# Late modulation tiles moved to the input projection's end, a rotation one product later, and the first up-weight casts ahead of the last squares

## The chip, the cores and the metric

The kernel runs on one core of one Trainium2 chip. The metric is device time in microseconds (us), the median of several executions; lower is better. Engines go by the names of the profile: PE (TensorE, matrix products and transposes), DVE (VectorE), ACT (ScalarE), POOL (GpSimd), SP (SyncE, which here only starts transfers). Each engine takes its instructions strictly in the order in which they were written into its queue, and an instruction that waits for another engine or for a transfer holds up everything behind it on its own engine.

## The reference

One block of a hybrid network on 512 latent tokens of width 2048 and 256 context tokens, everything in f32. Cut to what this change touches:

```
mod = silu(c) @ w_ada + b_ada                 # 6 vectors of 2048: the modulation
h   = rms_norm(x) * (1 + sc_a) + sh_a
p   = h @ w_in                                # input projection: q_a, kv_a, k_rope, conv columns
q   = rms_norm(q_a) @ w_q_b                   # 8 heads: 128 plain + 64 rotated columns
k,v = rms_norm(kv_a) @ w_kv_b                 # and the same for the context tokens
att = softmax(q k^T * scale) v                # 768 keys: 512 latent, 256 context
mix = group rms_norm(concat(att, gated conv))
x   = x + gt_a * (mix @ w_out)                # output projection, residual
hf  = rms_norm(x) * (1 + sc_f) + sh_f
u   = dwconv3(hf @ w_up);  x = x + gt_f * ((a * silu(g)) @ w_down)
```

The modulation's later vectors (`gt_a`, `sh_f`, `sc_f`, `gt_f`) are not needed before the output projection's residual.

## The kernel before, in words

Activations lie transposed, 128 features on the partitions and tokens along the free axis. PE multiplies a reduced-precision f32 kind, so each operand is split into a high and a low part and each product is three matmuls (`mm3`, lines 189, 190 and 191: high times high, high times low, low times high). A weight block is therefore loaded by SP into a raw tile, its high part is made by a cast on ACT (line 168) and its low part by a subtraction on DVE (line 169). The line 191 matmul is the one that needs the low part.

**The stages**, in the time of the profiled execution: the input projection runs to about 390 us (weights `rw`, split into `w_0`, `w_4`, `w_8`; products `pp`); the queries of head pair 0 and the context tiles follow (raw weights `rq`, split parts `wq00`, `wq02`, `wq01`; raw `rc`, split parts `wc..`); attention runs from about 433 to 627 us; the output projection to about 810; then `up` begins with a part called `uf` (raw weights `ufr`, split parts `ufw0`, `ufw1`, ... and, for rows 3 to 5, `ufw_0`/`ufw_512`).

**Late modulation tiles.** `w_ada` comes in tiles of 128 x 2048, one for each 128 outputs. Tiles 32 to 87 of it are done late: a tile is loaded by `late_load`, and DVE multiplies it with `silu(c)` and sums, either as two halves (line 266, two instructions; a tile in the raw buffers `ra`) or at once (line 270; a tile in the buffers `ada`). `late_both` does the dot of the tile loaded last and loads the next. Before the change they are spread over the attention (one tile a step, tiles `ra`) and the output projection (tiles `ada`).

**Attention.** `steps` are the 32 pairs of a head and a group of 128 queries. Step n makes the scores of step n+2 (PE, `s`, lines 741 to 745), the row maximum of step n+2's scores (DVE `mn`, line 756), the exponentials of step n+1 (ACT `p`, line 759), the transposes of step n's exponentials (PE `t`, line 772; their high part by ACT into `pth`, line 775, their low part by DVE into `ptl`, line 776), and every second step the product with the values (PE `po`, lines 189 to 191), whose result ACT copies out (`o`, line 788). Sums, scalings and their broadcasts (PE `gb`, line 309; DVE `o`, line 814, and `acc`, line 384) are put between. In the last steps the first weights of the output projection (`ofr`, two loads at steps 29 and 30) are fetched and split (`ofw_0`, `ofw_4`, `ofw_8`), and tiles of x (`x`, line 820) are loaded.

**Rotation.** `q_nope(0, i)` makes one of pair 0's three query products; the third (i = 2, `pq` from `wq02`) is copied out by ACT as `xq` (line 663), then rotated: one PE product with a permutation matrix (`qr`, line 389) and DVE work. The order of the calls is i = 0, 2, 1.

**From the output projection to up.** The last two rows of the output are done in two halves of the tokens (`ol`, weights `o14..`, `o15..`). After each half `residual` adds the result to x (DVE, line 1004) and squares it (ACT `fq`, line 364; DVE `fq0t`, line 365). `rms_steps` turns the squares into the norm: matmuls `rs` over the squares (line 326), a root on ACT and a reciprocal on DVE (`rr`, lines 299 and 301), and a broadcast by transposes on PE (`rs`, line 309). `hf_tile` then makes up's operands `hf` (ACT lines 983, 986 and 965; DVE lines 982, 987 and 966).

**What sets the order.** The program is written as Python loops; a scheduler with a simulated timeline then decides the order on each engine. `keep` pins an instruction to its place in the program, and `tc.issue_after` adds a dependency that holds an instruction back until another one. Buffers come from pools with a fixed number of places, so a load also waits until the last readers of its place are done. Small generators (`bg`, `pump`) let background work be issued between products.

## Time and profile before

| | us |
|---|---|
| median of 3 runs | 2130.95 (2128.15 to 2133.67) |
| profiled execution, time | 2127.2 |
| profiled execution, span | 2125.4 |
| PE busy in the span | 2080.8 (98%) |
| DVE busy in the span | 1823.5 (86%) |
| ACT busy in the span | 1049.7 (49%) |

The span goes from the first to the last instruction, and 1.8 us of the execution's time lie around it. Sums below are made against the profiled execution; the median lies 3.75 us above it. PE is idle for 2125.4 - 2080.8 = 44.6 us in the whole span. A time in a row of the timeline is an instruction's start, the number behind it its duration, and a bracket names how long the engine had been idle before it and what ended that. Durations of matmuls overlap: the distance of two starts tells what one costs.

### The profile page before, as it was taken

The numbers are of one execution on the slowest core, as the hardware profiler recorded it, in microseconds if no ns is written. First come the engines' busy times: TensorE is split into PE (matmuls) and PEld (weight loads), VectorE is DVE, ScalarE is ACT, GpSimd is POOL, SyncE is SP. The second block draws the span as 40 slices with busy tenths as digits, with TensorE's granted clock in tenths as the row PEclk, the third lists the DMA queues.
The fourth block names the chain that finished last, engine by engine and source line by source line (L and its number), as shares of the span: only waits on it lengthen the run. The fifth ranks groups of instructions, "written<-read, shape, count | busy, mean of one in ns | idle before, by whom it ended". The sixth has DMA issues, their size and how long they took to land.

```text
span 2125.4 us, 35175 instructions
## 1 busy us (share of the span) xinstructions
PE 2080.8 (98%) x13268; PEld 1873.8 (88%) x13268; DVE 1823.5 (86%) x2952; ACT 1049.7 (49%) x1715; POOL 116.7 (5%) x144
## 2 busy tenths in 40 slices
PE   7999999999989999999999999999999999999997
PEld 4788788889978889999999999999999889999997
DVE  7998987778897878898999999999999759888887
ACT  5533333555552337565555555555555433333445
POOL 0000000000000000011000000000000000000000
PEclk9999999999999999999999999999999999999999
DMA  9979885345558966587788788788788989877684
GB/s 329 349 275 325 277 273 192 127 143 194 207 219 318 351 254 183 143 218 205 230 240 235 225 238 237 228 236 240 225 232 246 336 309 308 261 233 235 207 248 139
DMA packets 165135, 513.74 MB, mean 242 GB/s; under 512 B 18402, under 2 KB 22754, under 8 KB 154850
## 3 DMA queue, kind: packets, MB, share of 16 engines
q1 hardware_dynamic: 128324, 418.14, 57.8%
q0 software_dynamic: 17408, 59.25, 14.2%
q10 hardware_dynamic: 19232, 34.09, 4.2%
q8 instruction: 104, 1.70, 0.3%
q14 instruction: 67, 0.55, 0.1%
HBM read 464.22 MB, written 46.14 MB: 240 GB/s over the span
## 4 chain that ended last, share of the span: by engine, by line
PE 94%; DVE 2%; ACT 2%; DMA 2%; issue 0%; SPq 0%; DVEq 0%; ACTq 0%
PE pp L189 4%; PE pp L191 4%; PE pp L190 4%; PE o L190 1%; PE o L189 1%; PE o L191 1%; PE d L189 1%; PE d L190 1%; PE d L191 1%; PE uf L189 1%; PE uf L191 1%; PE uf L190 1%; PE of L189 1%; PE of L190 1%; PE of L191 1%; PE pf L190 1%
## 5 line engine op out<-in xcount | busy, mean ns | idle before, releaser
L1167 POOL DMA_DIRECT2D u_s<-in_w_up x80 | 68.6, 857 | 682.2 <-DMA u_s<-in_w_up 312.2
L168 ACT CAST w_0h<-rw 128x512 fp32r<-128x512 f32 (+1 forms) x63 | 38.5, 618 | 108.4 <-PE pp L190 64.6
L270 DVE SCALAR_TENSOR_TENSOR ada<-ada,sv 128x2048 f32<-128x2048 f32 x32 | 73.3, 2289 | 19.7 <-DMA ada<-in_w_ada 19.7
L243 DVE SCALAR_TENSOR_TENSOR ada<-ada,sv 128x1024 f32<-128x1024 f32 x64 | 77.6, 1220 | 3.5 <-DMA ada<-in_w_ada 3.5
L540 DVE SCALAR_TENSOR_TENSOR ada<-ada,svc 128x1024 f32<-128x1024 f32 x64 | 76.0, 1221 | 2.8 <-DMA ada<-in_w_ada 2.7
L169 DVE TENSOR_TENSOR w_0l<-rw,w_0h 128x512 fp32r<-128x512 f32 (+1 forms) x63 | 42.7, 684 | 20.6 <-ACT w_0h L168 20.5
L266 DVE SCALAR_TENSOR_TENSOR ra<-ra,sv 128x1024 f32<-128x1024 f32 x48 | 57.0, 1218 | 0.1
L1281 DVE TENSOR_TENSOR u<-u,u_s 128x1024 f32<-128x1024 f32 x40 | 48.8, 1219 | 1.4 <-DMA u_s<-in_w_up 1.3
L1282 DVE TENSOR_TENSOR u<-u,u 128x1024 f32<-128x1024 f32 x40 | 48.7, 1217 | 0.0
L804 POOL TENSOR_TENSOR gr<-gr,half 128x8 f32<-128x8 f32 x4 | 9.6, 2390 | 631.0 <-DVE gr L803 631.0
L1091 DVE TENSOR_TENSOR tp<-a,tp 128x256 fp32r<-128x256 f32 x90 | 37.7, 419 | 3.0 <-ACT tp L1090 3.0
L775 ACT CAST pth<-t 128x384 fp32r<-128x384 f32 x64 | 28.9, 485 | 20.7 <-PE t L772 20.7
L1090 ACT CAST tp<-a 128x256 fp32r<-128x256 f32 x90 | 35.7, 404 | 5.2 <-DMA yl6h<-y_d 3.9
L1054 ACT ACTIVATE g<-g 128x512 f32<-128x512 f32 x43 | 27.3, 634 | 18.2 <-DVE g L1048 17.9
L551 DVE TENSOR_TENSOR acc<-acc,pp 128x512 f32<-128x512 f32 x50 | 34.2, 684 | 2.1 <-PE pp L191 2.1
L776 DVE TENSOR_TENSOR ptl<-t,pth 128x384 fp32r<-128x384 f32 x64 | 33.2, 550 | 2.3 <-ACT pth L775 2.2
L756 DVE TENSOR_REDUCE mn<-s 128x1 f32<-128x768 f32 x32 | 30.4, 952 | 4.4 <-PE s L745 4.4
L1046 ACT ACTIVATE g<-cg,sm 128x512 f32<-128x512 f32 x40 | 32.6, 816 | 0.0
L1046 ACT ACTIVATE a<-ca,sm 128x512 f32<-128x512 f32 x40 | 32.1, 802 | 0.0
L759 ACT ACTIVATE p<-s,mn 128x768 f32<-128x768 f32 x32 | 29.3, 914 | 3.3 <-DVE mn L756 2.9
L1047 DVE SCALAR_TENSOR_TENSOR g<-cg,sm,g 128x511 f32<-128x511 f32 x40 | 29.8, 745 | 0.0
L1048 DVE SCALAR_TENSOR_TENSOR g<-cg,sm,g 128x511 f32<-128x511 f32 x40 | 29.8, 745 | 0.0
(10238 smaller groups left out, 8906.4 us busy)
## 6 DMA issues: line engine op xcount, KB each, us to landing
ada<-in_w_ada SPq DMA_DIRECT2D x128, 512.0 KB, 5.7
u<-in_w_up SPq DMA_DIRECT2D x120, 512.0 KB, 8.9
w<-t_d SPq DMA_DIRECT2D x161, 256.0 KB, 5.3
u_s<-in_w_up SPq DMA_DIRECT2D x80, 512.0 KB, 3.9
u_s<-in_w_up POOLq DMA_DIRECT2D x80, 512.0 KB, 9.6
ada<-in_w_ada SPq DMA_DIRECT2D x32, 1024.0 KB, 7.0
t_d<-tp ACTq DMA_DIRECT2D x126, 256.0 KB, 5.9
v<-in_w_dnw SPq DMA_DIRECT2D x72, 384.0 KB, 5.3
```

The source lines that it names most:

```text
L169: V.tensor_tensor(out=lo[:, :n], in0=raw[:, a:a + n], in1=hi[:, :n].bitcast(F32), op=ALU.subtract)
L189: PE.matmul(ps, w[0], x[0], start=first, stop=False, skip_group_check=on_top)
L190: PE.matmul(ps, w[0], x[1], start=False, stop=False, skip_group_check=on_top)
L191: PE.matmul(ps, w[1], x[0], start=False, stop=last, skip_group_check=on_top)
L243: V.scalar_tensor_tensor(out=r, in0=r, scalar=1.0, in1=vec[:, i * 1024:(i + 1) * 1024], op0=ALU.mult, op1=ALU.mult, accum_out=col[:, i:i + 1])
L266: keep(V.scalar_tensor_tensor(out=halves[i], in0=halves[i], scalar=1.0, in1=svs[i], op0=ALU.mult, op1=ALU.mult, accum_out=lc[:, t % 4:t % ...
L270: keep(V.scalar_tensor_tensor(out=r, in0=r, scalar=1.0, in1=sv, op0=ALU.mult, op1=ALU.mult, accum_out=mod[:, t:t + 1]))
L540: keep(V.scalar_tensor_tensor(out=raw[q], in0=raw[q], scalar=1.0, in1=svc[:, q * 1024:(q + 1) * 1024], op0=ALU.mult, op1=ALU.mult, accum_o ...
L1046: A.activation(u, src, AF.Identity, bias=s("fb", m), scale=s("fw", 86 + m))
L1167: G_.dma_start(r[-1], src[more], accum_op=ALU.add)
L1281: V.tensor_tensor(out=a11, in0=a11, in1=s1, op=ALU.add)
L1282: V.tensor_tensor(out=a12, in0=a12, in1=a11, op=ALU.add)
```

## The change

Five edits:

- Two late tiles are loaded and done in the last part of the input projection (steps i = 20, 21, 22 of its third pass), as halves in buffers of their own (`ae`).
- In attention, late tiles are loaded up to step 24 only (before: up to step 27), so three tiles fewer are done there. Two are the ones above; one more falls to the output projection, whose late work is held back until the last `ptl` subtraction.
- The rotation of pair 0 is called after all three query products (i = 0, 2, 1), not inside the second.
- `residual` of the last half row is held behind the first casts of up's weights and behind an earlier `hf` tile; the norm's last squares and root are written after the first two rows of up's weights, and the `rs` matmuls are pinned in their place.
- The split parts of up's first three rows get their places before the loads are written (`pair4`).

```diff
@@ rms_steps
-    def rms_steps(sqs, n, a, width, dst, wait=0, one=False, hold=False):
+    def rms_steps(sqs, n, a, width, dst, wait=None, one=False, hold=False, pin=False):
...
+                if pin:
+                    keep(ins)
@@ input projection, third pass
+                    if 20 <= i <= 22:
+                        late_both((lambda t: ada_tiles(p_sb, 4, w_ada[t], f"ae{t}")) if i < 22 else None)
@@ q_nope
             A.copy(out=xq, in_=ps)
+            if pr:
+                q_rope(pr, xq)
+            else:
+                q_rope_0.append(xq)
+
+        q_rope_0 = []
+
+        def q_rope(pr, xq):
             rope(xq, sml(f"qr{pr}"), f"qr{pr}")
...
         for i in (0, 2, 1):
             q_nope(0, i)
+        q_rope(0, q_rope_0[0])
@@ attention steps
-            elif (at >= 2 or n >= 24) and n < 28:
+            elif (at >= 2 or n == 24) and n <= 24:
                 late_load(ada_raw)
@@ output projection, rows from OUT_EARLY on
-        late_both(ada_spare)
+        with tc.issue_after(ptl_last[0]) if k == OUT_EARLY else ExitStack():
+            late_both(ada_spare)
@@ last half rows
-            residual(NK - 2 + i, whole(raws[i], mix, f"o{NK - 2 + i}{h}", pso[i], HS[h], ld=ada_spare), HS[h])
+            ps = whole(raws[i], mix, f"o{NK - 2 + i}{h}", pso[i], HS[h], ld=ada_spare)
+            if (h, i) != (1, 1):
+                residual(NK - 2 + i, ps, HS[h])
+        if h == 1:
+            break
...
@@ up's first rows
+    pair_of = {}
+    for k in range(3):
+        pair_of[k] = pair4(f"ufw{k}")
...
-    held = [first_weights(k, k > 2) for k in range(EARLY)]
-    for k in range(3, EARLY):
-        hf_tile(k, H0)
+    held = [first_weights(k) for k in range(2)]
+    first_two = last_hi[0], last_lo[0]
+    with tc.issue_after(last_hi[0]), tc.issue_after(hf_last[0]):
+        residual(NK - 1, ps, HS[1])
+    one_bank[0] = in_turn([6])
+    bg.append(rms_steps(fsq, D, T // 2, T // 2, rl, wait=(1, 1), one=True, pin=True))
+    held += [first_weights(k, k > 2) for k in range(2, EARLY)]
+    with tc.issue_after(first_two[0]), tc.issue_after(first_two[1]):
+        for k in range(3, EARLY):
+            hf_tile(k, H0)
```

From line 300 on, line numbers in the rows of the changed kernel are larger by 4 to 27 than those of the same code before. In the rows below a name with a number behind an underscore is one buffer; `x3` at a row's end stands for three alike in a row.

**Input projection's end, DVE.** Before, from the first split of the last weight tile (`w_30`) to the low part of the first query weight (`wq00l`):

```order
L169 TENSOR_TENSOR w_30_0l<-rw_30_3298,w_30_0h 128x512
L348 TENSOR_TENSOR qa2l<-acc_574,qa2h 128x512
L551 TENSOR_TENSOR acc_686<-acc_686,pp_28_3203 128x512
L348 TENSOR_TENSOR qa3l<-acc_583,qa3h 128x512
L169 TENSOR_TENSOR w_30_4l<-rw_30_3298,w_30_4h 128x512
L354 TENSOR_TENSOR hc_3294<-cr_3291,hc_3294 128x256
L525 TENSOR_TENSOR cr_3361<-cg_3355,rc 128x256
L525 TENSOR_TENSOR cr_3367<-cg_3355,rc 128x256
L169 TENSOR_TENSOR w_30_8l<-rw_30_3298,w_30_8h 128x256
L354 TENSOR_TENSOR hc_3364<-cr_3361,hc_3364 128x256
L169 TENSOR_TENSOR wq00l<-rq_3413,wq00h 128x512
```

And the same place now, from the first low part of the normed `q_a` (`qa0l`):

```order
L352 TENSOR_TENSOR qa0l<-acc_529,qa0h 128x512
L266 SCALAR_TENSOR_TENSOR ae_3185,mod<-ae_3185,sv 128x1024
L266 SCALAR_TENSOR_TENSOR ae_3187,lc<-ae_3187,sv 128x1024
L169 TENSOR_TENSOR w_30_4l<-rw_30_3310,w_30_4h 128x512
L352 TENSOR_TENSOR qa1l<-acc_537,qa1h 128x512
L352 TENSOR_TENSOR qa2l<-acc_574,qa2h 128x512
L352 TENSOR_TENSOR qa3l<-acc_583,qa3h 128x512
L169 TENSOR_TENSOR w_30_8l<-rw_30_3310,w_30_8h 128x256
L358 TENSOR_TENSOR hc_3306<-cr_3303,hc_3306 128x256
L529 TENSOR_TENSOR cr_3373<-cg_3367,rc 128x256
L529 TENSOR_TENSOR cr_3379<-cg_3367,rc 128x256
L169 TENSOR_TENSOR wq00l<-rq_3425,wq00h 128x512
```

One pair of dots stands here, the other pair stands earlier, right behind the addition of `pp_27`; both are ahead of `wq00l`, and one `hc` moved behind it.

**The same place, ACT.** Before, around the copy of the product to be rotated (`xq`) and the casts of context weights (`wc_0h`):

```order
L347 CAST q00h<-pq_3423 128x512
L168 CAST wc_0h<-rc_3530 128x512 x3
L663 COPY xq_3457<-pq_3444 128x512
L347 CAST qro0h<-xq_3457 128x512
L168 CAST wc_0h<-rc_3530 128x512
L347 CAST q01h<-pq_3477 128x512
```

Now:

```order
L168 CAST wc_0h<-rc_3542 128x512
L530 ACTIVATE cr_3415<-cr_3415,modc,scc_3407 128x256
L357 CAST hc_3412<-cr_3409 128x256
L357 CAST hc_3418<-cr_3415 128x256
L351 CAST q00h<-pq_3435 128x512
L168 CAST wc_0h<-rc_3542 128x512
L669 COPY xq_3469<-pq_3456 128x512
L351 CAST q01h<-pq_3475 128x512
```

Before, three of the four casts from one context tile stand ahead of `xq`; now all four do.

**Attention's end, ACT.** Before, from the output copy (`o`) that the profile shows at about 600 us:

```order
L788 COPY o_5715<-po_5716 128x256
L775 CAST pth_5689<-t_5757 128x3x128
L775 CAST pth_5689<-t_5763 128x3x128
L759 ACTIVATE p_5794,den_5520<-s_5770,mn_5792 128x768
L775 CAST pth_5796<-t_5798 128x3x128
L775 CAST pth_5796<-t_5804 128x3x128
L759 ACTIVATE p_5847,den_5520<-s_5811,mn_5845 128x768
```

Now, from the same copy:

```order
L804 COPY o_5724<-po_5725 128x256
L168 CAST ofw_0h<-ofr_5876 128x512
L168 CAST ofw_4h<-ofr_5876 128x512
L168 CAST ofw_8h<-ofr_5876 128x512
L168 CAST ofw_0h<-ofr_5917 128x512
L791 CAST pth_5699<-t_5763 128x3x128
L791 CAST pth_5699<-t_5769 128x3x128
L773 ACTIVATE p_5796,den_5534<-s_5775,mn_5794 128x768
```

Four casts of output weights, which before stood behind the last `p` and two more `pth`, are now ahead of the casts and the exponentials of three steps. On DVE `ofw_0l` and `ofw_4l` stand likewise ahead of the row maximum of the step before the last, and `ofw_8l` and the next `ofw_0l` ahead of the `ptl` behind it.

**Up's start, ACT.** Before, from the cast of the third operand:

```order
L986 CAST hf2h<-x_4957 128x256
L983 ACTIVATE x_5008<-x_5008,mod,fs_7562 128x256
L364 ACTIVATE fq_7494<-x_5790 128x256
L983 ACTIVATE x_5104<-x_5104,mod,fs_7571 128x256
L1039 CAST ufw0h<-ufr_7514 128x768
L299 ACTIVATE rr<-rs,eps 128x2
L1039 CAST ufw1h<-ufr_7520 128x768
```

Now:

```order
L1003 CAST hf2h<-x_4969 128x256
L1062 CAST ufw0h<-ufr_7519 128x768
L1062 CAST ufw1h<-ufr_7523 128x768
L368 ACTIVATE fq_7528<-x_5792 128x256
L1062 CAST ufw2h<-ufr_7532 128x768
L1000 ACTIVATE x_5020<-x_5020,mod,fs_7566 128x256
L351 CAST ufw_0h<-ufr_7536 128x512
L1000 ACTIVATE x_5118<-x_5118,mod,fs_7575 128x256
L351 CAST ufw_512h<-ufr_7536 128x256
L351 CAST ufw_0h<-ufr_7546 128x512
L351 CAST ufw_512h<-ufr_7546 128x256
L351 CAST ufw_0h<-ufr_7556 128x512
```

The casts `ufw0h` and `ufw1h` come right behind `hf2h`, and the root `rr` now stands one row behind this, past the casts of rows 3 to 5. On PE the four `rs` matmuls over the squares, which stood ahead of the first `uf` product, now stand inside the third row of them, and both broadcasts behind that row.

More of the change, by code (lines that the diff above doesn't have):

```diff
@@ L310, in spread @@
         return ins.ins
-    def rms_steps(sqs, n, a, width, dst, wait=0, one=False, hold=False):
+    def rms_steps(sqs, n, a, width, dst, wait=None, one=False, hold=False, pin=False):
+        wait = wait or (0, 0)
         ng = width // P
@@ L320, in rms_steps @@
             pb = ps[:, 256:]
-        for _ in range(wait):
+        for _ in range(wait[0]):
             yield
@@ L330, in rms_steps @@
         rsqrt(r, ps[:, :ng], n)
-        for _ in range(wait):
+        for _ in range(wait[1]):
             yield
@@ L760, in softmax @@
             return pt
+        ptl_last = []
         def transposes(st, pt):
@@ L775, in transposes @@
                 A.copy(out=hi, in_=trv)
-                V.tensor_tensor(out=ptl[:, 3 * u:3 * u + 3, bs], in0=trv, in1=hi.bitcast(F32), op=ALU.subtract)
+                ptl_last[:] = [V.tensor_tensor(out=ptl[:, 3 * u:3 * u + 3, bs], in0=trv, in1=hi.bitcast(F32), op=ALU.subtract).ins]
         def attend(hd, half):
@@ L1019, in block_kernel @@
         for i in range(2):
-            residual(NK - 2 + i, whole(raws[i], mix, f"o{NK - 2 + i}{h}", pso[i], HS[h], ld=ada_spare), HS[h])
+            ps = whole(raws[i], mix, f"o{NK - 2 + i}{h}", pso[i], HS[h], ld=ada_spare)
[3 more added lines that the diff above has]
+            break
         one_bank[0] = in_turn([6 * h])
-        bg.append(rms_steps(fsq, D, h * T // 2, T // 2, rl, wait=2, one=True))
-        if h == 0:
-            bg.append(hf_early())
+        bg.append(rms_steps(fsq, D, h * T // 2, T // 2, rl, wait=(2, 2), one=True))
+        bg.append(hf_early())
     assert late["t"] == late["end"] and late["raw"] is None
@@ L1034, in block_kernel, with pair4, split4 @@
     last_hi, last_lo = [], []
-    def split4(src, n, nm):
-        hi = rw.tile([P, 1024], F32R, tag="wh", bufs=3, name=nm + "h")
-        lo = rw.tile([P, 1024], F32R, tag="wl", bufs=3, name=nm + "l")
+    def pair4(nm):
+        return [rw.tile([P, 1024], F32R, tag="w" + z, bufs=3, name=nm + z) for z in "hl"]
+    def split4(src, n, nm, pair=None):
+        hi, lo = pair or pair4(nm)
         last_hi[:] = [A.copy(out=hi[:, :n], in_=src).ins]
@@ L1155, in first_weights @@
             return [part(w[g // 4], g % 4) for g in range(G)]
-        w = split4(raw[:, :G * P], G * P, f"ufw{k}")
+        w = split4(raw[:, :G * P], G * P, f"ufw{k}", pair_of.pop(k, None))
         return [part(w, g) for g in range(G)]
@@ L1552, in block_kernel @@
     sqs.append(add_squares(None, acc2[zb.m + 1][:, H0], T // 2, "eqb", a=0))
-    bg.append(rms_steps(sqs, D, 0, T // 2, rl, wait=1, one=True, hold=True))
+    bg.append(rms_steps(sqs, D, 0, T // 2, rl, wait=(1, 1), one=True, hold=True))
     outs = final(0, rl[:, HS[0]])
```

## The prediction

> **What bounds the kernel now.** I read the page's engine line first, then PE's waits, then windows and timelines around the places that the change touches.
>
> ```profile
> PE 2080.8 (98%) x13268; PEld 1873.8 (88%) x13268; DVE 1823.5 (86%) x2952; ACT 1049.7 (49%) x1715; POOL 116.7 (5%) x144
> ...
> PE po L189 <- DVE ptl L776: 5.3, 2, 3.1
> ...
> 610.00:620.00 10.00, 6.92 (x41) 6.11 (x41) 9.26 (x20) 5.96 (x13) 0.00 (x0) 0.83 0.60 195
> 620.00:630.00 10.00, 6.88 (x38) 6.39 (x37) 8.93 (x16) 8.01 (x17) 0.00 (x0) 0.83 0.38 134
> ```
>
> PE bounds the kernel: it is idle for 44.6 us of 2125.4. No edit takes a product away, so only these idle times and slow clock can change. Behind the span, PE, weight loads, DVE and ACT busy, the window rows give the granted clock: in the 20 us around attention's end PE is busy for 6.9 of 10, its clock is 0.83, and DVE is busy for 9 of 10. PE's largest wait, on `ptl`, lies there. That is the place with most to win; waits on `xq` and on the last squares, quoted below, are the other two targets.
>
> **Attention's end.** The next rows are from the timelines of PE, ACT and DVE, from the chain of waits, and from the view of the tile `ofr`.
>
> ```profile
> 601.33 1.04 PE L309 MATMUL gb<-io,gr 128*128 128x128 f32 x8
> ...
> 603.20 0.65 PE L309 MATMUL gb<-io,gn 128*128 128x128 f32 x4 [0.18 <-DVE o L814]
> 604.54 0.50 PE L741 MATMUL s<-kl31h,q31h 128*128 128x512 f32 x1 [0.69 <-ACT p L759]
> ...
> 609.32 1.17 PE L772 MATMUL t<-io,p 128*128 128x128 f32 x6
> 611.36 0.65 PE L309 MATMUL gb<-io,gn 128*128 128x128 f32 x4 [0.88 <-DVE ptl L776]
> ...
> 615.05 0.39 PE L189 MATMUL po<-pth,v30h 128*128 128x256 f32 x1 [2.21 <-DVE ptl L776]
> ...
> 616.87 0.41 PE L189 MATMUL po<-pth,v32h 128*128 128x256 f32 x1
> 617.09 0.41 PE L190 MATMUL po<-ptl,v32h 128*128 128x256 f32 x1
> ...
> 623.24 0.55 PE L189 MATMUL po<-pth,v30h 128*128 128x256 f32 x1 [3.12 <-DVE ptl L776]
> ```
>
> ```profile
> 599.79 0.37 ACT L788 COPY o<-po 128x256 f32<-128x256 f32 x1 [2.35 <-PE po L191]
> 602.73 0.86 ACT L775 CAST pth<-t 128x384 fp32r<-128x384 f32 x2 [2.57 <-PE t L772]
> ```
>
> ```profile
> 593.66 1.22 DVE L266 SCALAR_TENSOR_TENSOR ra<-ra,sv 128x1024 f32<-128x1024 f32 x1
> ...
> 602.41 0.74 DVE L814 SCALAR_TENSOR_TENSOR o<-o,sm,gb 128x512 f32<-128x512 f32 x1
> ...
> 613.30 1.22 DVE L266 SCALAR_TENSOR_TENSOR ra<-ra,sv 128x1024 f32<-128x1024 f32 x1
> 614.44 0.55 DVE L776 TENSOR_TENSOR ptl<-t,pth 128x384 fp32r<-128x384 f32 x1
> ```
>
> ```profile
> 614.55 4.20 DMA ofr<-in_w_out_first
> ...
> 619.39 0.27 ACT o L788
> ...
> 621.37 0.60 DVE mx1l L348
> ...
> 622.63 0.48 DVE ptl L776
> ```
>
> ```profile
> DMA to landing us min/median/max: 4.3/5.5/8.0
> ```
>
> What goes: the idle of five waits, 0.18 + 0.69 + 0.88 + 2.21 + 3.12 = 7.1 us. With it goes the slow clock: from 616.2 to 620.1 and from 623.2 to 626.4, about 7.0 us of busy PE, a product of 256 columns starts 0.22 us after the one before (616.87, 617.09), against the 0.12 of the rows at 809 below. At 0.12 to 0.22 these 7.0 us hold 3.9 us of work, so 3.1 are lost. Together 10.2 us.
>
> What frees them: three tiles' dots, six instructions at 1.14 us (613.30 to 614.44) or 6.9 us of DVE, all ahead of the `ptl` that PE waits for.
>
> What comes instead: the `ofr` loads now wait for dots that end earlier, and their casts stand ahead of attention's own work on ACT and DVE. I lay this on the times of before. Both dots of the last tile now stand where one stood (593.66), so everything behind 594.80 starts 1.14 later, and the first `ofr` is issued at 596.0; at 4.25 us (the 4.20 row, the 4.3 of the tile view) it has landed at 600.3. Its three casts (0.52 each, by the ACT rows of the rotation below) end by 601.9, ahead of the `pth` casts of 602.73. The second `ofr` waits for the next dot, to about 598.7; it lands at 603.0 and its cast holds ACT to 603.6, so the two `pth` and the `p` behind it come 0.9 us late. On DVE two low parts (0.60 each, as `mx1l`) begin when the first cast is through (600.9) and end at 602.1; the row maximum and the third low part bring it to 603.6, where `o` begins, 1.2 us later than 602.41. So `gb` waits 0.18 + 1.2 = 1.4, and `s`, with `p` 0.9 late, 0.5 behind it.
>
> Then the tail. At 611.36 and 615.05 the dots were the last to come (613.30 and 614.44 are the end of that chain); without them I leave 0.6 of 3.1. The last wait's chain goes from the output copy at 619.39 to the end of `ptl` at 623.11, 3.7 us, and only `mx1l` leaves it: 3.1, under which PE has ten transposes and broadcasts, 1.2 us at a product's 0.12: 1.9 remain. New idle: 1.4 + 0.5 + 0.6 + 1.9 = 4.4; each of the four waits adds some 0.15 for the signal between engines (`hf2h` to `ufw0h` to `uf` below: 811.24 + 0.81 = 812.05 and 812.11 is the least of it), so I take 5.0. **Gain 10.2 - 5.0 = 5.2 us.** The bounds: without the new waits at the two early places it is 7.1; with a landing of 8.0 in place of 4.25 it is 5.2 - 3.75 = 1.5.
>
> The third tile goes to the output projection, one dot among DVE work that its consumers need 2 us or more later: 0. If that cover were gone it would cost its 2.3 us.
>
> **Input projection's end.**
>
> ```profile
> 379.50 0.43 DVE L169 TENSOR_TENSOR w_8l<-rw,w_8h 128x256 fp32r<-128x256 f32 x1 [0.58 <-PE pp L191]
> ...
> 388.91 0.43 DVE L354 TENSOR_TENSOR hc<-cr,hc 128x256 fp32r<-128x256 f32 x1 [0.79 <-ACT hc L353]
> 389.61 0.69 DVE L169 TENSOR_TENSOR wq00l<-rq,wq00h 128x512 fp32r<-128x512 f32 x1 [0.27 <-ACT wq00h L168]
> ...
> 391.75 0.39 PE L191 MATMUL pq<-qa0h,wq00l 128*128 128x512 f32 x1
> ```
>
> Four dots, 4 x 1.14 = 4.6 us, stand ahead of `wq00l`. DVE can swallow its idle there, 0.58 + 0.79 + 0.27 = 1.6, and 0.4 of an `hc` that moved behind. So `wq00l` ends at 390.30 + 4.6 - 2.0 = 392.9, and PE wants it at 391.75: **loss 1.1 us** (0.5 to 1.6; nothing more, as the `w_8l` of the last tile is used only behind this product). The added loads stand ahead of weight loads that have places to spare: 0.
>
> **Rotation.**
>
> ```profile
> 403.79 0.62 ACT L168 CAST wc_0h<-rc 128x512 fp32r<-128x512 f32 x1 [1.70 <-PE pq L190]
> 404.31 0.58 ACT L663 COPY xq<-pq 128x512 f32<-128x512 f32 x1
> ...
> 404.94 1.13 PE L389 MATMUL qr<-xq,kc 128*128 128x512 f32 x2 [0.97 <-ACT xq L663]
> ```
>
> `xq` is late not because its product is, but because a context cast ahead of it on ACT waits until a product has left that cast's place. Now the fourth cast stands ahead of `xq`, and the place that it takes is left by the third product (`wq01`), the one that was to cover the rotation. So `xq` again comes about 1 us after the last product: **gain 0**. If the scheduler's places let that cast through, the gain is 0.97.
>
> In pair 3 the same order slips in: the cast `wq31h` moves ahead of its `xq`.
>
> ```profile
> 552.03 0.59 ACT L663 COPY xq<-pq 128x512 f32<-128x512 f32 x1 [1.31 <-PE pq L191]
> ...
> 553.56 1.02 PE L389 MATMUL qr<-xq,kc 128*128 128x512 f32 x2
> ```
>
> `xq` had 0.9 us to spare; the cast alone (0.52) would fit in that, its load, if it is not there yet, would not. Between 0 and 0.8: **loss 0.4**.
>
> **Up's start.**
>
> ```profile
> 809.11 0.28 PE L190 MATMUL ol<-mx15l,o151w1536h 128*128 128x256 f32 x1
> 809.23 0.28 PE L191 MATMUL ol<-mx15h,o151w1536l 128*128 128x256 f32 x1
> 811.15 0.61 PE L326 MATMUL rs<-io,fq0t 128*128 128x1 f32 x4 [1.65 <-DVE fq0t L365]
> 812.11 0.39 PE L189 MATMUL uf<-hf0h,ufw0h 128*128 128x256 f32 x1 [0.34 <-ACT ufw0h L1039]
> ```
>
> ```profile
> 808.99 0.41 ACT L986 CAST hf2h<-x 128x256 fp32r<-128x256 f32 x1
> ...
> 811.24 0.81 ACT L1039 CAST ufw0h<-ufr 128x768 fp32r<-128x768 f32 x1
> ```
>
> ```profile
> DMA to landing us min/median/max: 3.1/4.2/6.9
> ```
>
> Idle here is 1.65 + 0.34 = 2.0. Now `ufw0h` follows `hf2h`, so it runs its 0.81 from 809.3 on and the first `uf` starts at 810.15, with 0.65 us idle behind the last product (809.51): gain 1.35. The `rs` products run later, with their squares long there: 0. **Gain 1.3 us.** Against it stands the load of row 3: it now waits for the last product of the output projection (809.5), which it did not before. At `ufr`'s median landing of 4.2 it is there at 813.9. The root stands behind five of these rows' casts (three of 0.52, two of 0.31): 816.1, and 816.8 with the root and its reciprocal. PE comes to the broadcasts after 54 products of 0.12 and the `rs`, at 810.15 + 6.5 + 0.4 = 817.0. So each us of a later landing costs nearly one; at the longest, 6.9, the gain is 1.35 - 2.5 = -1.1. I take the median's.
>
> **Sum.** -5.2 (attention) + 1.1 (`wq00l`) + 0 (rotation) + 0.4 (pair 3) - 1.3 (up) = -5.0 us: profiled execution 2127.2 - 5.0 = 2122.2, and, the median being 3.75 above it, **2125.95, say 2126**.
>
> **The rivals.**
> 1. *The clock still falls.* Before, 5.7 us without a product (609.32 to 615.05: transposes, broadcasts, waits) were followed by half clock; the 3.2 us from 601.3 to 604.5 were not. Now that second stretch grows by 1.2 + (0.5 - 0.69), to some 4.2 us: a fraction (4.2 - 3.2)/(5.7 - 3.2) = 0.4 of the way. Half clock lasted 3.1 us after products began again (623.24 to 626.4), and half of that is lost: +1.6, so 2127.6. Chance 0.25.
> 2. *The new waits do not come*, `ofr` landing before its casts' turn, and `wq00l` finds its idle: -5.0 - 1.9 - 1.1 = -8, 2123. For it: both loads are issued early, and less `ra` traffic runs beside them. Against it: the order of the casts, which makes every late byte a wait. Chance 0.18.
> 3. *Slower: in-order ACT behind `ofr`.* The four casts hold `pth` and `p` of three steps. If `ofr` takes the 8.0 us of its longest landing, PE idles 3.75 more, in one stretch of over 5.7 us, and the 3.1 us of slow clock come back: -5.0 + 6.85 = +1.9, 2133. It decides from a landing of about 6.2 us on, where 1.9 more of waiting and the clock's 3.1 take up the 5.0. For it: the median of all eight `ofr` loads, 5.5, is above the 4.25 that I took. Against: the three `ra` loads that ran here are the ones removed. Chance 0.08.
> 4. *The tail is not DVE's.* At the waits of 615.05 and 623.24 ACT's and DVE's own chain takes the dots' place, and 3 of the 5.2 us stay: 2129. Chance 0.12. That leaves 0.37 for the forecast as it stands, 2123.5 to 2128.5 with its bounds.
>
> To the first: the Trainium skill, page "TensorE: Matmul & The Clock Gate", section "Part 1: The HAM clock gate", says that activity is judged in free-running windows of 3.4 us and that a whole idle window halves the clock; its Part 4 says that transposes do not count as activity. The trace agrees: transposes alone held no clock at 609, and 3.2 us were too short. By that rule a 4.2 us stretch would hold a whole window with an estimated chance of (4.2 - 3.4)/3.4 = 0.24, close to the rival's.
>
> **Chances and range.** What a measurement of this kernel can tell from no change is about 0.3%, 6.4 us, so faster begins at 2124.6. The forecast lies 1.4 us above that: with a third of its own cases below, all but a little of rival 2 and nothing else, faster has 0.12 + 0.16 + 0.04 for the scatter of the runs shown (5.5 us wide) = 0.32. Slower needs rival 3 and scatter beside it: 0.06. The same: 0.62. The range goes from rival 2 less 3 us of scatter, 2120, to rival 3, 2133.
>
> **What would show it.** Right: DVE without `ra` dots in the last 12 us of attention; waits of `po` on `ptl` there under 2.5 us in all; new waits of `gb` on `o` and of `s` on `p` of 1 to 2 us together; granted clock 1.00 in the window of the last 20 us (0.8 for rival 1); a wait of about 1 us on `wq00l`; `qr` still waiting about 1 us for `xq`; first `uf` within 1 us of the last `ol`. Wrong: casts `ofw_0h` waiting over 3 us on the load, a wait of `uf` in its fourth row, or lost time in stages that the change does not name.

## The result, and the profile after

The changed kernel takes 2125.44 us (median of 21 executions, 2121.05 to 2130.21), the kernel before, beside it, 2130.10 us (median of 21). The ratio is 0.9977 with a 95% interval from 0.9969 to 0.9985: 4.9 us faster, 3.2 to 6.6. Measured once more with the experiments it was 0.9963 (0.9951 to 0.9975). The forecast was 2126, 5.0 us less than before. One execution of the kernel before took 11052.76 us; ratios compare fast executions alone, so it does not count. The interval leaves out 1, so the kernel is faster, by 0.23%; that is under the 0.3% which the prediction took as the least that can be told from no change, as forecast. The second, 0.37%, is just past it.

These are the first line of the page of the changed kernel, and from PE's waits those at the places of the prediction (us in total, times, longest).

```profile
PE 2081.7 (98%) x13268; PEld 1872.2 (88%) x13268; DVE 1820.7 (86%) x2951; ACT 1045.5 (49%) x1715; POOL 116.7 (5%) x144
```

```profile
PE gb L309 <- DVE o L830: 1.4, 1, 1.4
PE s L755 <- ACT p L773: 1.3, 3, 0.5
...
PE ol L189 <- DVE x L1021: 1.2, 1, 1.2
PE po L190 <- DVE ptl L792: 1.1, 1, 1.1
...
PE qr L393 <- ACT xq L669: 1.0, 1, 1.0
...
PE pq L191 <- DVE wq00l L169: 0.8, 1, 0.8
PE uf L189 <- ACT ufw0h L1062: 0.7, 1, 0.7
```

The 5.3 us of `po` on `ptl` have become 1.1, and the 1.6 of `rs` on the last squares are gone. `gb` on `o` (1.4), `ol` on `x` (1.2), `wq00l` (0.8) and `uf` on its cast (0.7) have come in their place; `qr` on `xq` stands where it stood.

The windows around attention's end show the same (columns as before: busy time of PE, weight loads, DVE, ACT, POOL, then the granted clock):

```profile
600.00:610.00 10.00, 8.23 (x47) 7.08 (x46) 7.88 (x12) 4.71 (x11) 0.46 (x1) 0.83 0.63 210
610.00:620.00 10.00, 8.37 (x66) 7.49 (x66) 6.50 (x15) 8.03 (x20) 0.00 (x0) 1.00 0.01 2
620.00:630.00 10.00, 10.00 (x60) 8.78 (x59) 10.00 (x16) 7.53 (x15) 0.00 (x0) 1.00 0.55 210
```

From 610 to 620 us DVE is busy for 6.50 of 10 us, where it was for 9.26 before, and from 620 on PE is busy all the time; but the clock is 0.83 in the first window, where it was 1.00 before. The timelines of PE, then ACT and DVE, tell what happens in it:

```profile
601.53 1.03 PE L309 MATMUL gb<-io,gr 128*128 128x128 f32 x8
...
604.58 0.65 PE L309 MATMUL gb<-io,gn 128*128 128x128 f32 x4 [1.35 <-DVE o L830]
605.65 0.69 PE L755 MATMUL s<-kl31h,q31h 128*128 128x512 f32 x1 [0.42 <-ACT p L773]
606.14 0.63 PE L756 MATMUL s<-kl31l,q31h 128*128 128x512 f32 x1
606.57 0.63 PE L757 MATMUL s<-kl31h,q31l 128*128 128x512 f32 x1
...
614.25 0.36 PE L189 MATMUL po<-pth,v30h 128*128 128x256 f32 x1 [0.20 <-DVE acc L388]
...
617.99 0.38 PE L189 MATMUL po<-pth,v30h 128*128 128x256 f32 x1 [0.27 <-ACT pth L791]
619.46 0.39 PE L190 MATMUL po<-ptl,v30h 128*128 128x256 f32 x1 [1.09 <-DVE ptl L792]
```

```profile
603.33 0.62 ACT L168 CAST ofw_0h<-ofr 128x512 fp32r<-128x512 f32 x1 [1.21 <-DMA ofr<-in_w_out_first]
603.85 0.85 ACT L791 CAST pth<-t 128x384 fp32r<-128x384 f32 x2
```

```profile
601.11 0.69 DVE L169 TENSOR_TENSOR ofw_0l<-ofr,ofw_0h 128x512 fp32r<-128x512 f32 x1 [0.33 <-ACT ofw_0h L168]
...
603.78 1.40 DVE L830 SCALAR_TENSOR_TENSOR o<-o,sm,gb 128x512 f32<-128x512 f32 x2
```

ACT waits 1.21 us for the second `ofr` load with `pth` behind it; DVE does two output weights ahead of `o`; PE waits 1.35 and 0.42 us. From 601.53 to 605.65, 4.1 us, it has only broadcasts, transposes and waits, and the products that follow are 0.43 us apart (606.14, 606.57), where at full clock this distance is 0.23 (608.20 and 608.43 in the second execution below).

To compare stages I cut each trace at PE's first instruction of a kind: the last `gp` of the input projection (390.39 us before, 388.63 after), the first `s` of attention, the first `po` with the values of the last pair of heads (`v30h`; 597.45, 597.65), the first `of`, the first `ol`, the first `uf` and the fifth row of `uf` (its operand is `hf4`). The lengths in us between these, worked out from the starts, for all kernels of this study; in the last column the pieces of half clock (granted clock 0.50) at attention's end, each 3.4 us long:

| kernel | `gp` to `s` | to `po` | to `of` | to `ol` | to `uf` | to `hf4` | sum | pieces |
|---|---|---|---|---|---|---|---|---|
| before | 43.4 | 163.7 | 30.2 | 158.0 | 26.4 | 8.9 | 430.6 | 2 |
| the change | 44.4 | 164.7 | 24.8 | 158.0 | 26.5 | 9.7 | 427.9 | 1 |
| the change, second execution | 44.5 | 164.3 | 23.1 | 158.0 | 25.8 | 9.6 | 425.2 | 0 |
| late tiles alone | 47.1 | 165.3 | 24.7 | 158.0 | 29.3 | 10.4 | 434.8 | 1 |
| up's start alone | 43.4 | 163.6 | 30.4 | 159.6 | 24.5 | 9.6 | 431.1 | 4 |
| rotation alone | 42.1 | 163.7 | 29.1 | 158.0 | 26.4 | 8.9 | 428.2 | 2 |
| rotation and up's start | 42.1 | 163.7 | 27.7 | 158.0 | 24.5 | 9.7 | 425.6 | 1 |
| change, `xq` ahead | 43.4 | 164.0 | 23.1 | 158.6 | 24.3 | 9.7 | 423.0 | 0 |
| change, tiles earlier | 42.1 | 164.2 | 23.2 | 158.0 | 25.4 | 9.7 | 422.4 | 0 |
| change, second `ofr` cast held | 44.4 | 165.2 | 22.7 | 158.6 | 24.3 | 9.6 | 424.8 | 0 |
| change, four `ofr` casts held | 44.4 | 164.2 | 25.2 | 158.6 | 24.3 | 9.6 | 426.2 | 1 |
| change, third tile kept | 44.4 | 165.2 | 23.7 | 158.0 | 24.5 | 9.7 | 425.4 | 0 |
| three improvements | 42.1 | 164.1 | 22.7 | 158.0 | 25.3 | 9.8 | 422.0 | 0 |
| three improvements, second execution | 42.1 | 164.8 | 22.7 | 158.0 | 26.0 | 9.8 | 423.3 | 0 |

Ahead of `gp` the executions differ by 3.8 us (388.4 to 392.2), also between two of the same kernel (388.6 and 391.2 for the change). Three executions have a piece of half clock there: the change's second, late tiles alone, and the second `ofr` cast held. Of the 3.7 us by which the profiled span of the change is shorter, 1.8 lie ahead of `gp`; as its second execution is there 0.8 us later than the kernel before, I count them as spread. The stages give 2.7, and 0.8 is lost again behind `hf4`, in stages that the change does not touch (1305.2 us to the end of the span, 1304.4 before, 1306.0 in the second execution); 0.6 of that 0.8 is the slower pace that the last section shows.

### The profile page after: what moved, and what is told of

It reads as the page before. It is cut to its first block, busy times and chain, and to the rows that moved or that the text cites. A ratio compares the mean times of both kernels' runs of the same rounds, so it can differ in the third digit from the quotient of the medians.

```text
span 2121.7 us, 35173 instructions
## 1 busy us (share of the span) xinstructions
PE 2081.7 (98%) x13268; PEld 1872.2 (88%) x13268; DVE 1820.7 (86%) x2951; ACT 1045.5 (49%) x1715; POOL 116.7 (5%) x144
## 4 chain that ended last, share of the span: by engine, by line
PE 88%; DMA 5%; DVE 4%; ACT 2%; issue 1%; SPq 0%; DVEq 0%; ACTq 0%
PE pp L189 4%; PE pp L191 4%; PE pp L190 4%; DMA ada<-in_w_ada 3%; PE d L189 1%; PE d L191 1%; PE d L190 1%; PE of L191 1%; PE of L189 1%; PE of L190 1%; PE pf L190 1%; PE pf L191 1%; PE pf L189 1%; PE uf L189 1%; PE uf L191 1%
## 5 line engine op out<-in xcount | busy, mean ns | idle before, releaser
L270 DVE SCALAR_TENSOR_TENSOR ada<-ada,sv 128x2048 f32<-128x2048 f32 x33 | 75.6, 2291 | 24.7 <-DMA ada<-in_w_ada 24.7
L266 DVE SCALAR_TENSOR_TENSOR ra<-ra,sv 128x1024 f32<-128x1024 f32 x42 | 49.8, 1218 | 0.1
L770 DVE TENSOR_REDUCE mn<-s 128x1 f32<-128x768 f32 x32 | 30.4, 952 | 6.2 <-PE s L759 6.0
L368 ACT ACTIVATE fq<-x 128x512 f32<-128x512 f32 (+1 forms) x17 | 9.9, 582 | 45.4 <-DVE x L1021 45.3
L773 ACT ACTIVATE p<-s,mn 128x768 f32<-128x768 f32 x32 | 29.3, 915 | 4.4 <-DVE mn L770 4.1
L1070 DVE SCALAR_TENSOR_TENSOR g<-cg,sm,g 128x511 f32<-128x511 f32 x40 | 29.8, 746 | 0.0
```

The source lines that it names most:

```text
L266: keep(V.scalar_tensor_tensor(out=halves[i], in0=halves[i], scalar=1.0, in1=svs[i], op0=ALU.mult, op1=ALU.mult, accum_out=lc[:, t % 4:t % ...
L270: keep(V.scalar_tensor_tensor(out=r, in0=r, scalar=1.0, in1=sv, op0=ALU.mult, op1=ALU.mult, accum_out=mod[:, t:t + 1]))
```

## The experiments

**The change a second time.** Nothing is edited.

> The changed kernel once more, for a second profiled execution. Theory A (half clock at attention's end depends on where the stretch without products falls in a fixed raster, not on the kernel alone): the same waits at the same rows (gb on o 1.4, s on p 0.4, qr on xq 1.0, wq00l 0.8), but the place and number of half-clock pieces may differ from the first execution's single one; stage lengths from the first of product to the first up row within 0.3 us of it, attention's end from 23.1 (none) to 24.8 us (one piece). Theory B (the half clock belongs to the kernel): one piece of 3.4 us at the same row again. Ratio to before 0.9977 within 0.001.

Ratio 0.9963 (0.9951 to 0.9975). The waits are the same: `gb` 1.34, `s` 0.36, `qr` 1.0, `wq00l` 0.8. But the clock is not. Here are the window of the first execution in which these products lie, and that of the second with its rows of PE:

```profile
605.60:609.00 3.40, 3.35 (x11) 2.87 (x12) 1.77 (x4) 0.00 (x0) 0.00 (x0) 0.53 0.49 202
```

```profile
607.90:611.30 3.40, 3.40 (x24) 3.19 (x25) 3.13 (x7) 1.05 (x3) 0.00 (x0) 1.00 0.51 210
...
606.86 0.65 PE L309 MATMUL gb<-io,gn 128*128 128x128 f32 x4 [1.34 <-DVE o L830]
607.87 0.49 PE L755 MATMUL s<-kl31h,q31h 128*128 128x512 f32 x1 [0.36 <-ACT p L773]
608.20 0.39 PE L756 MATMUL s<-kl31l,q31h 128*128 128x512 f32 x1
608.43 0.40 PE L757 MATMUL s<-kl31h,q31l 128*128 128x512 f32 x1
```

The stretch without products is followed by half clock (0.53 over 3.4 us) in one and by full clock in the other. Theory A holds: whether the piece comes is not decided by the kernel alone. The raster can be read too: in late tiles alone, the next experiment, the pieces start at 83.79, 612.85 and 817.65 us, and the distances are 155 and 60 times 3.413 us. A piece costs 24.75 - 23.10 = 1.65 us. Of the five profiled executions that have this stretch (the change twice, late tiles alone, `xq` ahead, tiles earlier) two had it.

**Late tiles alone.** The edits of `late_both`, the attention's steps and the output projection are made, those of the rotation and of up are not.

```diff
+                    if 20 <= i <= 22:
+                        late_both((lambda t: ada_tiles(p_sb, 4, w_ada[t], f"ae{t}")) if i < 22 else None)
...
-            elif (at >= 2 or n >= 24) and n < 28:
+            elif (at >= 2 or n == 24) and n <= 24:
...
-        late_both(ada_spare)
+        with tc.issue_after(ptl_last[0]) if k == OUT_EARLY else ExitStack():
+            late_both(ada_spare)
```

> The kernel before with the late tiles' move alone (two early ones, three fewer in attention, one more in the output projection); rotation and up's start as before. Theory A (the sum of the prediction, corrected by the profile after): attention's end gives 5.2 to 5.5, the wait on wq00l takes 0.8, the waits of p and kl30l in pairs 2 and 3 take 1.0, and the tile added to the output projection takes 1.4 to 2.0 where the residual's DVE row stands behind its dot: 1.5 to 2 us faster than before in all. Theory B (the extra dot in the output projection costs nothing, its wait in the profile after belongs to the new start of up): 3.5 us faster, and no wait of ol on x in the trace.

Ratio 0.9992 (0.9982 to 1.0001), 1.7 us. That is the figure of theory A, and the wait of `ol` on `x` rules out theory B; but the trace does not add up to it, its stages being 4.2 us longer than before. Attention's end is 5.6 us shorter, with one piece of half clock. The output projection's last rows (`ol` to `uf`) are 2.9 us longer: `ol` waits 2.1 us on `x`. What theory A does not have is the rotation's wait, 2.75 us in place of 0.97, and a piece of half clock at up's start (817.65), where `uf` to `hf4` is 1.5 us longer. The profiled execution took 2137.01 us, the longest of the twelve and 7.9 above their median, so its rows say more than its sum. PE, ACT:

```profile
409.59 1.12 PE L389 MATMUL qr<-xq,kc 128*128 128x512 f32 x2 [2.75 <-ACT xq L665]
```

```profile
406.36 0.60 ACT L526 ACTIVATE cr<-cr,modc,scc 128x256 f32<-128x256 f32 x1 [1.88 <-DVE cr L525]
406.87 0.60 ACT L168 CAST wc_0h<-rc 128x512 fp32r<-128x512 f32 x1
...
408.96 0.57 ACT L665 COPY xq<-pq 128x512 f32<-128x512 f32 x1
```

The four dots make DVE late by some 2 us, not only for `wq00l`: a context row `cr` on ACT waits 1.88 us for DVE, and `xq` stands behind it.

**Rotation alone.**

```diff
             A.copy(out=xq, in_=ps)
+            if pr:
+                q_rope(pr, xq)
+            else:
+                q_rope_0.append(xq)
+
+        q_rope_0 = []
+
+        def q_rope(pr, xq):
             rope(xq, sml(f"qr{pr}"), f"qr{pr}")
...
         for i in (0, 2, 1):
             q_nope(0, i)
+        q_rope(0, q_rope_0[0])
```

> The kernel before with the rotation a product later, alone. Theory A (what holds xq is the fourth context cast that stands ahead of it on ACT, and that order comes only with the early late tiles; alone, the change leaves three casts ahead of xq): the wait of qr on xq goes, 1.0 us faster. Theory B (the rotation cannot be covered, xq being late for any order): qr waits 1.0 us again, no change.

Ratio 0.9975 (0.9966 to 0.9985), 5.3 us. In the trace the wait is gone, as theory A says: the fourth context cast is behind `xq`.

```profile
404.51 0.58 ACT L663 COPY xq<-pq 128x512 f32<-128x512 f32 x1
406.78 0.62 ACT L168 CAST wc_0h<-rc 128x512 fp32r<-128x512 f32 x1 [1.69 <-PE pq L190]
```

```profile
406.81 1.02 PE L389 MATMUL qr<-xq,kc 128*128 128x512 f32 x2
...
620.64 0.36 PE L189 MATMUL po<-pth,v30h 128*128 128x256 f32 x1 [1.68 <-DVE acc L384]
```

But the size is five times what was expected. The stages give 1.4 us up to `s`, and 1.1 at attention's end, where the scheduler now puts the low part `mx1l` behind the last two `ptl` on DVE, so that the last `po` waits 1.68 us (620.64) in place of 3.12: 2.4 in all. For the rest see the clock, below.

**Up's start alone.** The edits of the last half rows, `rms_steps` and up's first rows are made, the others are not.

> The kernel before with up's first casts ahead of the last squares alone. Theory A: 1.2 us faster, all between the last ol product and the fourth uf row; no wait of ol on x, attention's end as before (waits of 6 to 7 us, two half-clock stretches). Theory B (up's start brings the wait of ol on x and pays for itself): within 0.3 us of before.

Ratio 0.9990 (0.9979 to 1.0000), 2.1 us. From `ol` to the fifth row it is 26.4 + 8.9 - 24.5 - 9.6 = 1.2 us shorter, with no wait of `ol` on `x`: theory A. The `uf` products come 1.9 us earlier, and 0.7 of it is given back behind them, where `rs` and the broadcasts now stand. The rest of the measured 2.1 lies within the interval. The sum of all stages is 0.5 us longer than before: this execution has four pieces of half clock in place of two, and one of them runs into the output projection (159.6 in place of 158.0).

**`xq` ahead of the fourth cast**, in the changed kernel.

```diff
-            A.copy(out=xq, in_=ps)
+            xq_ins[:] = [A.copy(out=xq, in_=ps).ins]
...
             for a in range(0, NK, 4):
-                for q, w in enumerate(blocks(raw, 4, f"wc{i}{a}", a)):
+                with tc.issue_after(xq_ins[0]) if (i, a) == (0, 12) else ExitStack():
+                    ws = blocks(raw, 4, f"wc{i}{a}", a)
+                for q, w in enumerate(ws):
```

> The changed kernel with the fourth cast of the first context tile held behind the copy xq. Theory A: the wait of qr on xq goes (1.0 us faster than the changed kernel, 5.9 faster than before), and the cast still waits for the same product. Theory B (the copy is late for another reason, or the context product then waits for that cast): qr or pc waits about 1 us, no change against the changed kernel.

Ratio to before 0.9954 (0.9942 to 0.9967). `qr` waits no more, and no context product waits instead; `gp` to `s` is 43.4 against 44.4: theory A, 1.0 us. The time is 9.8 us below before, where 5.9 was expected. In this trace `ol` does not wait on `x` either (`ol` to `uf` 24.3), which is not the work of this edit alone: see the third tile, below.

```profile
406.47 0.58 ACT L669 COPY xq<-pq 128x512 f32<-128x512 f32 x1
406.95 0.62 ACT L168 CAST wc_0h<-rc 128x512 fp32r<-128x512 f32 x1
```

```profile
407.10 1.12 PE L393 MATMUL qr<-xq,kc 128*128 128x512 f32 x2
```

**The two early tiles four products earlier.**

```diff
-                    if 20 <= i <= 22:
-                        late_both((...) if i < 22 else None)
+                    if 16 <= i <= 18:
+                        late_both((...) if i < 18 else None)
```

> The changed kernel with the two early late tiles four products earlier (steps 16 to 18 of the last pass). Theory A (DVE is short of idle only just ahead of wq00l): the 0.8 us wait on wq00l goes, and, the queue of ACT falling differently, the copy xq comes ahead of the fourth context cast and its 1.0 us wait goes too: 2 to 3 us faster than the changed kernel, about 7 to 8 faster than before. Theory B (the dots cost PE their time wherever they stand in the input projection): the wait turns up at another low part, pp on w_0l or w_4l, and nothing is won.

`wq00l` starts at 387.58 and PE uses it at 389.72, with no wait; `xq` is again ahead of the fourth cast, and `qr` does not wait either. `gp` to `s` is 42.1 us against 44.4: 2.3 us, theory A.

```profile
387.58 0.69 DVE L169 TENSOR_TENSOR wq00l<-rq,wq00h 128x512 fp32r<-128x512 f32 x1 [0.44 <-ACT wq00h L168]
```

```profile
389.72 0.39 PE L191 MATMUL pq<-qa0h,wq00l 128*128 128x512 f32 x1
```

The timing does not show it: 0.9966 (0.9956 to 0.9977) against 0.9963 for the changed kernel in the same comparison. Two us are less than these intervals can tell.

**The second `ofr` cast held** behind the last exponentials (`p_last`).

```diff
+            p_last[:] = [A.activation(pt, ss[:, :768], AF.Exp, bias=mn, scale=-1.0, accum_out=den[hd // 2][:, i:i + 1]).ins]
...
-                w = row_weights(w_out_first, k, "of", raw=out_raw[k])
+                with tc.issue_after(p_last[0]) if k == 2 else ExitStack():
+                    w = row_weights(w_out_first, k, "of", raw=out_raw[k])
```

> The changed kernel with the casts of the second ofr load held behind the last exponentials. Theory A (ACT stands for that load ahead of pth and p): ACT's wait of 1.2 us on ofr goes, s waits 0.4 less on p, attention's end is 0.4 to 0.9 us shorter at the same clock. Theory B (DVE's rows around o set that end, ACT has room): gb waits the same 1.4 us, s waits on, and the casts lengthen the tail: no change or up to 0.5 slower.

Ratio 0.9959 (0.9947 to 0.9971). ACT's wait on the load is gone and attention's end is 0.4 us shorter than without half clock before (22.7 against 23.1): the lower end of theory A. But `s` does not wait less. The broadcasts moved away from ahead of it, and one wait of 1.5 replaces 1.35 and 0.42:

```profile
607.12 0.50 PE L755 MATMUL s<-kl31h,q31h 128*128 128x512 f32 x1 [1.52 <-ACT p L773]
```

The stage ahead (`s` to `po`) is 165.2, 0.5 to 0.9 longer than in the change, so the sum, 424.8 against 425.2, and the ratio tell no gain.

**All four `ofr` casts held** (the same edit with `k < 4`).

> The changed kernel with all four early ofr casts held behind the last exponentials. Theory A (they stand in the way only by the wait for the second load): attention's end as long as with that load's cast alone held, 22.7 us from the last heads' first value product to the first output product. Theory B (what is taken out of the way early comes back in the tail, where ACT and DVE make the last transposes' parts): gb waits under 0.5, the last po waits 1.5 to 2.5 in place of 1.4, the stage 23 to 23.7 us without half clock; no gain.

Ratio 0.9987 (0.9978 to 0.9997): slower than the change by the middle, though the interval overlaps that of the change's first measurement. Theory B: `gb` waits 0.18, as before the change, and the tail takes it back, with 2.7 at the last `po` and 0.85 at a transpose. With one piece of half clock, which begins in the tail's stretch of 5.2 us without a product, the stage has 25.2 us; without the 1.65 of a piece that would be 23.6.

```profile
604.26 0.65 PE L309 MATMUL gb<-io,gn 128*128 128x128 f32 x4 [0.18 <-DVE o L830]
...
619.37 0.55 PE L189 MATMUL po<-pth,v30h 128*128 128x256 f32 x1 [2.70 <-DVE ptl L792]
```

So the casts in the middle of attention's steps are not a mistake of the change: they must be made somewhere, and for the first load's three the tail is the dearer place.

**The third tile kept in attention.**

```diff
-            elif (at >= 2 or n == 24) and n <= 24:
+            elif (at >= 2 or n in (24, 25)) and n <= 25:
```

> The changed kernel with late tiles loaded up to step 25 of attention, so that the third tile stays there and none is added to the output projection. Theory A (the added tile's dot, and the load that it waits for, hold the residual's row on DVE and through it ol on PE): no wait of ol on x, from the first ol to the first up product 24.3 to 24.5 us in place of 25.4 to 26.5; attention's end pays for one more pair of dots, 0.5 to 1.5 us; in all within 1 us of the changed kernel. Theory B (the wait of ol comes from the transfers there, whatever the number of tiles): ol still waits about 1 us.

`ol` no longer waits, and `ol` to `uf` is 24.5 us, as with up's start alone, against 26.5 and 25.8: theory A, and the added tile had cost 1.3 to 2.0 us there. What it did can be read in the changed kernel, on DVE and PE:

```profile
790.45 2.29 DVE L270 SCALAR_TENSOR_TENSOR ada<-ada,sv 128x2048 f32<-128x2048 f32 x1 [1.10 <-DMA ada<-in_w_ada]
...
793.27 0.48 DVE L1021 SCALAR_TENSOR_TENSOR x<-ol,mod,x 128x256 f32<-128x256 f32 x1
```

```profile
793.89 0.36 PE L189 MATMUL ol<-mx0h,o141w0h 128*128 128x256 f32 x1 [1.17 <-DVE x L1021]
```

The dot waits 1.10 us for its load and takes 2.29; the residual's row stands behind it, and PE cannot begin the next half row before that row has read the first one's sums.

It is the late load that makes this dear, and not the dot as such. Three kernels have the added tile too, and no wait of `ol` on `x`: `xq` ahead, the second `ofr` cast held and all four held. In the change the tile's load is issued 4.7 us behind the first `ol` (780.40) and lands 9.95 behind it, and the dot follows at 10.05. In `xq` ahead it is issued 2.0 us ahead of the first `ol` (778.76), and the dot, without a wait, starts 4.25 behind it:

```profile
783.01 2.29 DVE L270 SCALAR_TENSOR_TENSOR ada<-ada,sv 128x2048 f32<-128x2048 f32 x1
```

There `ol` to `uf` is 24.3 and the stage ahead 0.6 us longer. Why the load is issued earlier in these three is not shown; their edits lie elsewhere.

In attention the tile costs 0.6 us at the end (23.7). The stage ahead is 165.2 as well, but so it is with the second `ofr` cast held, without that tile. The ratio, 0.9980 (0.9972 to 0.9989), is not better than the change's.

**Rotation and up's start without the late tiles' move.**

> The kernel before with the rotation and up's start changed, and the late tiles left where they were. Theory A (parts add where they do not meet on one queue): the wait of qr gone (1.0, with 0.4 at the context tiles), 1.1 at attention's end as with the rotation alone, 1.2 at up's start: 3.5 to 4 us faster than before. Theory B (the late tiles bring most of the gain): 2 us faster than before at most.

Ratio 0.9967 (0.9954 to 0.9980), 7.0 us, and in the stages 430.6 - 425.6 = 5.0, of which 1.65 are a piece of half clock less: theory A for the rest. Within the intervals this is as fast as the whole change. By the stages it has 425.6 with one piece of half clock, the change 427.9 with one and 425.2 with none. No gain of the late tiles' move, which the prediction put first, can be told beside the two small edits.

**Three improvements together**: the tiles earlier, the fourth cast behind `xq`, the second `ofr` cast held.

> The changed kernel with all three: early tiles four products earlier, the fourth context cast behind xq, the second ofr casts behind the last exponentials. Theory A: the sum of the single ones, 3 to 4 us faster than the changed kernel, 8 to 9 faster than before. Theory B (the first two take away the same wait, the third is nothing): 2 us faster than the changed kernel.

> The three improvements together once more (early tiles four products earlier, the fourth context cast behind xq, the second ofr casts behind the last exponentials). Theory A: ratio to before 0.9953 again within 0.001, and stage lengths as in its first execution. Theory B (the first time was the spread of its executions): ratio 0.997, that of the changed kernel.

Ratios 0.9953 (0.9941 to 0.9965) and 0.9955 (0.9939 to 0.9970), medians 2122.18 and 2120.79 us: 9.6 to 10 us faster than before, and the second execution confirms the first. Against the change the two theories of the first run are not told apart: the stages give 2 to 6 us (422.0 and 423.3 against 427.9 and 425.2), the ratios 2 to 5, and in the comparison that has both kernels it is 2 (0.9953 against 0.9963). The rows speak for the first half of theory B: `gp` to `s` is 42.1, as with the tiles earlier alone, so `xq` ahead adds nothing to that. The third edit gives 0.4 at attention's end. The interval does not overlap that of the change's first measurement in the first case and touches it in the second, and it overlaps that of the second measurement.

## Why the prediction was right, point by point

**Attention's end: -5.2 predicted, -5.5 in the profiled execution.** The new waits came where and as large as worked out: `gb` on `o` 1.35 (1.4 predicted), `s` on `p` 0.42 (0.5), the second `ofr` landing at 603.3 (603.0). The tail was sized too long: 0.20 where 0.6 was left, and 0.27 + 1.09 = 1.36 where 1.9 was, and the 0.6 added for signals was not there: 3.3 us of idle against 5.0. That 1.7 us was taken by something else, the half clock of rival 1, 1.65. The mechanism was right; that the number was too is luck, because two errors met. Without a piece of half clock the gain is 7.1 us. The prediction has 7.1 as its upper bound, but for the case that the two early waits do not come, and they came.

**Rival 1** (the clock still falls) was given 0.25 and a price of 1.6; it happened in two of five executions, at 1.65. The quiet stretch was 4.1 us (4.2 predicted). The pieces of half clock are 3.413 us long, start whole multiples of that apart, and come or stay away at the same stretch of the same kernel. The Trainium skill, page "TensorE: Matmul & The Clock Gate", section "Part 1: The HAM clock gate", speaks of a window of 3413 ns that runs free. The traces agree in the length and the raster. How much of a window must be quiet no run here settles.

**The third tile: 0 predicted, 1.3 to 2.0 measured.** This is the step that failed: "one dot among DVE work that its consumers need 2 us or more later". The consumers were looked at, but not the row of the residual behind the dot, and not the dot's own wait for its load (1.10). Where the load comes early, as in `xq` ahead, the cost is some 0.6. The sentence on the price without cover (2.3) was near.

**`wq00l`: +1.1 predicted, +0.8 measured.** Right, and the wait was cheap to avoid: four products earlier DVE has the room.

**Rotation: 0 predicted, 0 measured** (0.97 and 0.96 us of wait). The reason given, the fourth cast ahead of `xq`, is shown by the kernel in which that cast is held (-1.0). It was not the whole reason: the dots make a context row `cr` late (ACT waits for it 1.88 us in late tiles alone, 1.87 in the change), and with the old place of the rotation the wait is 2.75 us. So by the stage from `gp` to `s` the move of the rotation is worth 2.8 us beside the early tiles (47.1 against 44.4) and 1.4 alone (43.4 against 42.1); it looks like nothing only because the early tiles took as much. The prediction took the edits one by one against the kernel before and did not see that they meet on ACT.

**Pair 3: +0.4 predicted.** The stage from `s` to `po` lost 1.0 and 0.6 us in the two executions. `qr` of pair 3 did not wait. A product of `wq31` waits 0.4 for `kl30l`, both times, and the first time `s` waits 0.4 for `p` in an earlier step. So the loss came at other rows than the one named, and it is half as large again or more.

**Up's start: -1.3 predicted, -1.2 measured** (up's start alone). The first `uf` came 0.67 us behind the last `ol` (0.65 predicted), and the load of row 3 was in time.

**The sum: -5.0 predicted, -4.9 measured**, -7.9 the second time. Summed over the stages the two profiled executions give -2.7 and -5.4. That the first measurement is within 0.1 us of the sum is luck: the third tile cost 1.3 to 2.0 us more than predicted, attention's idle came out 1.7 us shorter, a piece of half clock comes or goes with 1.65, and the two measurements differ by 3.

## What to carry to other kernels

An edit that frees an engine is worth the waits that its work was holding less the waits of whatever the scheduler moves into the room, and both can be read from the new order laid over the old times; here that gave two waits to within 0.1 us. Look at each queue that an added instruction stands in, and at every row behind it there, not at the consumers of its result only: the third tile's term was wrong, and the reason at `xq` incomplete, by rows behind an added dot. Look also at when the load of an added piece of work is issued: the same dot cost 1.3 to 2.0 us behind a late load, and some 0.6 behind an early one. Where several edits touch the same queues, take the edits in pairs as well: the small rotation edit is worth 1.4 us alone, 2.8 beside the early tiles, and its wait reads the same before and after.

## What was not expected of the hardware

The spread of one kernel's executions (2121 to 2130 for the change) has three parts that the traces show. One is the first 390 us, which take from 388.4 to 392.2. The second is the number of pieces of half clock. The third is the pace of PE in the last stage, the products `v` from about 1750 us on. In most executions these start 118.7 ns apart, but 120.0 in the whole stage of late tiles alone, from about 1780 on with the second `ofr` cast held, and from about 2030 on in the change's first execution: this costs 3.7, 3.6 and 0.6 us, with no wait that explains it and at a granted clock of 1.00. These are windows of the kernel before and of late tiles alone, with 676 and 669 matmuls in 80 us of busy PE:

```profile
1860.00:1940.00 80.00, 80.00 (x676) 80.00 (x676) 66.41 (x94) 31.66 (x38) 4.26 (x5) 1.00 0.80 237
```

```profile
1860.00:1940.00 80.00, 80.00 (x669) 80.00 (x668) 67.41 (x96) 30.95 (x37) 4.27 (x5) 1.00 0.76 228
```

What sets that pace is not shown; no experiment edits this stage.

The half clock can also be looked for in the means. Averaged over all timed executions of a comparison the granted clock was 0.9952 to 0.9956 for the kernel before, 0.9954 with up's start alone, 0.9962 with the late tiles alone, 0.9968 to 0.9970 for the change and for the rotation alone, 0.9966 with the tiles earlier, and 0.9972 to 0.9974 with the other improvements. A difference of 0.0015 in 2125 us is 3.2 us of full clock, if PE is busy in all of it. For the rotation alone that is about what its stages left open (5.3 measured, 2.4 in the trace), so I take the rest to be half clock that the profiled execution happened to have and the others did not; this is an inference from the means, no run shows it directly. The means also hold the last 9 to 13 us of each execution, where the clock is 0.50 in every trace; by the length of that end alone they can differ by 0.0009. If the inference is right, part of what a change of 1 us brings at a place where PE rests for 3 to 6 us is not that 1 us, but how often the clock falls there.
